# Homes of the large tiles: the same remainder modulo 128 in every pool

## The chip, the core and the metric

The kernel runs on one core of a Trainium2 chip. The metric is the device time of one execution in microseconds (us); lower is better. The core has TensorE (PE, matrix products; its weight loads are listed as PEld), VectorE (DVE), ScalarE (ACT), GpSimd (POOL) and the queues that issue DMA transfers (SP's above all). Operands lie in the on-chip memory SBUF, 128 partitions wide; a tile's home is the byte address in a partition at which it starts. Products land in the eight banks of PSUM.

## What is computed

A decoder trunk of two layers on x of shape (1, 512, 1024), all float32. Cut to what matters:

```python
def even_mixer(h, ...):                      # layer 0
    proj = h @ w_in; q, k, v, glu = split(proj)
    a = band_attention(rotary(q), rotary(k), v, window=127, sinks)   # 8 heads, 2 kv heads
    c = silu(layer_norm(causal_depthwise_conv(g_a * sigmoid(g_b)))) # 31 taps
    return concat([a, c]) @ w_out
def odd_mixer(h, ...):                       # layer 1
    proj = h @ w_in; q, k, v, z = split(proj)
    c_out = dilated attention, (window, dilation) (128,1), (512,4), (2048,16), mixed by denominators
    d_out = u * (spatial_w @ layer_norm(g) + spatial_b)             # u, g = split(gelu(z))
    return concat([c_out, d_out]) @ w_out
for layer in range(2):
    h = h + mixer[layer](rms_norm(h))
    h = h + (silu(n @ w_gate) * (n @ w_up)) @ w_down, n = rms_norm(h)   # 1024 -> 2816 -> 1024
return rms_norm(h)
```

## The kernel before

The residual h is kept as 8 tiles of 128 features x 512 tokens. Weights stream from memory in blocks of 128 x 1024 (raw). Each number is split in two parts of type float32r, a high and a low one: ACT writes the high part (w_hi, L174), DVE or POOL the difference (w_lo, L151). A product is three matmuls: high x high, low x high, high x low, with 512 columns moving and 128 x 128 stationary. `acc3` (L201 to L203) has the weights stationary (w_hi, w_lo) and the activations moving (xh, xl after a norm; oh, ol the mixer's output; hh, hl the FFN's hidden tiles; st and yc are homes that later oh and ol tiles reuse). `tok_gemm` (L262 to L264) has it the other way round. A weight load of the next matmul runs while the present one streams its columns.

The program's stages are: the first mixer (to about 196 us), the FFN of layer 0 (to about 560), the second mixer (to about 750), the FFN of layer 1 with the last norm. An FFN works in groups of four hidden tiles; the first group of two goes through `acc3`. For each of the later ones `product` makes seven products (a Strassen-like scheme) in which the weights' combination moves (w2h, w2l, L909 to L912) and the activations, either xh and xl or the prepared sums S1 to S4 (tiles s1 to s4), stand. Between the products stand down projections of the group before (`add_down`, 12 matmuls for each of 8 output tiles, result added to h in L939) and transposes (`turn`, L924) that need a PSUM bank which an add to h has to free. At the group's end ACT works a Silu (L997), then splits the next weights (L885), and DVE follows (L998, L151).

PE's order is written by hand: generators for attention and the conv's norm are stepped between matmuls by a clock of estimated costs (`C0`). The other engines' order is made by a scheduler from the order in which the code stands and from waits; equal code gives equal order.

Homes come from pools that are laid one behind the other in a partition: `const`, `keep` (h, xh, xl), `wpool` (raw, w_hi, w_lo), `scr` (scratch: ga, gb, small columns such as rl), and above them, one at a time, the pool of the stage: mix0, ffn, mix1. Each tile takes the next free place, rounded up to 32 bytes. The first large tiles lie at 96 above a multiple of 256. The stage pools begin at byte 111,392, which is 32 above a multiple of 256; in mix0 the score tiles Pm (two, of 8 rows of 257 columns) bring the tiles behind them to 160 above one.

Of the kernel before, what the change touches and what calls it, by code (L numbers as in the profile page):

```python
# [18 lines left out]
F32 = mybir.dt.float32  # L19
F32R = mybir.dt.float32r  # L20
AF = mybir.ActivationFunctionType
ALU = mybir.AluOpType

P = 128
# [110 lines left out]
def trunk_kernel(ctx: ExitStack, tc: tile.TileContext, xT, ws, cols, sinks, sgu_g, sgu_b,  # L135
                 spat_wT, spat_b, rope_c, rope_s, ident_d, mask0_d, mask1_d, fin_g, y):
    nc = tc.nc
    V, A, G, T = nc.vector, nc.scalar, nc.gpsimd, nc.tensor
# [5 lines left out]
    scr = ctx.enter_context(tc.tile_pool(name="scr", bufs=2))  # L144
    psum = ctx.enter_context(tc.tile_pool(name="psum", bufs=1, space=bass.MemoryType.PSUM))

    def bank(i, shape=None):
        return psum.tile(shape or [P, S], F32, name=f"bank{i}")
# [295 lines left out]
    with ExitStack() as mx:  # L444
        mp = mx.enter_context(tc.tile_pool(name="mix0", bufs=1))
# [5 lines left out]
        nc.sync.dma_start(sinkb, bass.AP(tensor=sinks.tensor, offset=sinks.offset, ap=[[0, P], [1, 8]]))  # L451
        nsink = mp.tile([P, 8], F32, name="nsink")
        V.tensor_scalar(out=nsink, in0=sinkb, scalar1=-1.0, scalar2=None, op0=ALU.mult)
        cp = [mp.tile([P, TAPS - 1 + S], F32, name=f"cp{j}") for j in range(4)]
        for j in range(4):
            G.memset(cp[j][:, 0:TAPS - 1], 0.0)
# [2 lines left out]
        V.tensor_scalar(out=taps, in0=taps, scalar1=0.5, scalar2=None, op0=ALU.mult)  # L459


        mp.tile([P, 8, 2 * P + 1], F32, name="Pm", bufs=2)
        for b in range(2):
            mp.tile([P, S], F32R, name=f"qs{b}", bufs=2)
        yc = [mp.tile([P, S], F32, name=f"yc{j}") for j in range(4)]
# [107 lines left out]
        def scores0(i):  # L573
            yield 0.0, C0["q"][i]
            while i >= 2 and ("V", i - 2) not in done:
                yield 0.0, 0.3
            qss = qTs[i]

            Pm = mp.tile([P, 8, 2 * P + 1], F32, name="Pm", bufs=2)
            A.activation(Pm[:, :, 2 * P:].rearrange("p (n b) o -> p n (b o)", b=2),  # L580
                         nsink[:, i:i + 5:4][:, None, :].to_broadcast([P, NQ, 2]), AF.Copy)
            nm = scr.tile([P, 8], F32, name="nm")
            l = scr.tile([P, 8], F32, name="l")
            for n2 in range(2):
                sb = [bank(2), bank(3)]
                for n1 in range(2):
                    n = 2 * n2 + n1
                    for b in range(2):
                        lo = max(n - 1, 0) * P
                        w = (n + 1) * P - lo  # L590
                        out = sb[b][:, n1 * 256 + 256 - w:n1 * 256 + 256]
                        q = slice(n * P, (n + 1) * P)
                        T.matmul(out, qss[b][:, q], khh[b][:, lo:lo + w], start=True, stop=False)
                        T.matmul(out, qss[b][:, q], kl[b][:, lo:lo + w], start=False, stop=True)
                for n1 in range(2):
                    n = 2 * n2 + n1
                    for b in range(2):
                        u = 2 * n + b
                        c0 = P if n == 0 else 0
                        hd = i + 4 * b  # L600
                        V.tensor_tensor_reduce(
                            out=Pm[:, u, c0:2 * P], in0=sb[b][:, n1 * 256 + c0:n1 * 256 + 256],
                            in1=mask0[:, c0:], scale=-0.125, scalar=nsink[:, hd:hd + 1],
                            op0=ALU.add, op1=ALU.min, accum_out=nm[:, u:u + 1])
                if n2 == 0:
                    yield 0.9, C0["S"]
            for u in range(8):
                c0 = P if u < 2 else 0
                A.activation(Pm[:, u, c0:], Pm[:, u, c0:], AF.Exp, bias=nm[:, u:u + 1], scale=-1.0,
                             accum_out=l[:, u:u + 1])  # L610
            rl = scr.tile([P, 8], F32, name="rl")
            V.reciprocal(rl, l)
            del qTs[i]
            pend[i] = Pm, rl, seq.t + 0.9 + C0["ST"]
            yield 0.9, 0.0
# [70 lines left out]
        for step in C0["steps"].split():  # L686
# [38 lines left out]
            if after:  # L725
                waiting.append(after)
                if len(waiting) > 1:
                    seq.until(lambda: "norm" in done)
                flush()
            elif kind == "L":  # L730
                seq.add("L", conv_norm())
            elif kind == "S":
                seq.add("S", scores0(i))
            elif kind == "V":
                seq.add("V", values0(i))
            elif kind == "Y":
                seq.until(lambda: all(("V", j) in done for j in range(4)))
                ps = bank(5)
                for k in range(4):
                    acc3(ps, (oh[k], ol[k]), k == 0, k == 3)  # L740
                early[i] = mp.tile([P, S], F32, name="prod", bufs=3)
                A.activation(early[i], ps, AF.Copy)
            else:
                if kind == "C":
                    break
                ns = {"A": C0["na"], "X": C0["nx"], "B": C0["na"] + C0["nx"]}[kind]
                k = i + 4 if kind == "B" else i
                seq.until(lambda: (("L" if kind == "B" else "V"), i) in done)
                for n in ns:
                    if n not in po:  # L750
                        po[n], ks[n] = bank(n), 0
                    ks[n] += 1
                    acc3(po[n], (oh[k], ol[k]), ks[n] == 1, ks[n] == 8)
# [313 lines left out]
    with ExitStack() as mx:  # L1067
        mp = mx.enter_context(tc.tile_pool(name="mix1", bufs=1))
# [67 lines left out]
        def scores1(i, qk, ql):  # L1136
            yield 0.0, C0["q1"]
            while i >= 2 and ("V1", i - 2) not in done:
                yield 0.0, 0.3
            Pm = [mp.tile([P, 10 * P], F32, name="Pm", bufs=3) for _ in range(2)]  # L1140
            nm = scr.tile([P, 8], F32, name="nm")
            rl = scr.tile([P, 8], F32, name="rl")
            for n in range(NQ):
                w = (n + 1) * P
                q = slice(n * P, w)
                sb = [bank(2), bank(3)]
                for b in range(2):
                    qs, ks = qk[b]
                    T.matmul(sb[b][:, :w], qs[:, q], ks[:, :w], start=True, stop=False)
                    T.matmul(sb[b][:, :w], ql[b][:, q], ks[:, :w], start=False, stop=True)  # L1150
                for b in range(2):
                    u = 2 * n + b
                    V.tensor_tensor_reduce(
                        out=Pm[b][:, offs[n]:offs[n] + w], in0=sb[b][:, :w],
                        in1=mask1[:, S - w:], scale=-0.125, scalar=3.0e38,
                        op0=ALU.add, op1=ALU.min, accum_out=nm[:, u:u + 1])
                    A.activation(Pm[b][:, offs[n]:offs[n] + w], Pm[b][:, offs[n]:offs[n] + w], AF.Exp,
                                 bias=nm[:, u:u + 1], scale=-1.0, accum_out=rl[:, u:u + 1])
                if n < NQ - 1:
                    yield 0.22 * (n + 1), C0["S1"]  # L1160
            V.reciprocal(rl, rl)
            pend[i] = Pm, rl, seq.t + 0.9 + C0["ST1"]
            yield 0.9, 0.0
# [22 lines left out]
        for i in range(4):  # L1186
            ps = gemm1(0)
            qT = mp.tile([P, S], F32, name="qT")
            rope(ps, qT, tabs)
            ps = gemm1(1)  # L1190
            kT = mp.tile([P, S], F32, name="kT")
            rope(ps, kT, tabs)
            seq.add("S1", scores1(i, *stack(i, qT, kT)))
            seq.add("V1", values1(i))
# [151 lines left out]
```

## Time and profile before

| | |
|---|---|
| runs | 1118.15, 1120.03, 1122.57 us; median 1120.03 |
| profiled execution | 1121.99 us, span 1120.3 us |
| mean granted clock of TensorE | 0.990 of full speed |
| busy: PE, DVE, ACT, POOL | 97%, 62%, 51%, 21% of the span |
| chain that ended last | PE 75%, DVE 11%, DMA 5%, ACT 4% |

Busy time is the time in which an engine works on at least one instruction. Matmuls are pipelined: each is shown for longer than it holds the array, so the distance between two starts is their pace, and the mean ns of a group goes up and down with it. In the table by stage each engine's busy time is followed by its count of instructions; behind the engines come the granted clock, the share of the 16 DMA engines and GB/s.

### The profile page before, as it was taken

What the parts mean: (1) busy time and instruction counts of PE and PEld (TensorE: products, weight loads), DVE (VectorE), ACT (ScalarE), POOL (GpSimd) and SP (SyncE); (2) the same over time, 40 slices, a digit from 0 to 9 for tenths busy, and PEclk for the clock granted to TensorE, in tenths of its full rate; (3) what the DMA queues carried; (4) which work ended last, traced back from release to release, by engine and by line L of the source; (5) the groups of instructions that cost most, each with busy time, mean ns of one, the idle gap of its engine ahead of it and who ended that gap; (6) DMA issues with size and microseconds to landing.
All of it is one profiled execution on the core that took longest, in us unless ns stands there. A gap on an engine that the chain in (4) does not pass through costs nothing.

```text
span 1120.3 us, 13714 instructions
## 1 busy us (share of the span) xinstructions
PE 1082.4 (97%) x5118; PEld 888.2 (79%) x5118; DVE 692.2 (62%) x1051; ACT 570.3 (51%) x930; POOL 233.3 (21%) x210
## 2 busy tenths in 40 slices
PE   9989889999999999999999999999999999999997
PEld 7877767878878888888887888787778788888785
DVE  3889966866565556564647647556665645555543
ACT  6577745754444353533546654446544443535433
POOL 0889944211101010100023300002111010101002
PEclk9989999999999999999998999999999999999999
DMA  6211113977767676611521111239877676666122
GB/s 230 69 57 62 46 57 112 273 204 179 187 151 167 175 150 188 135 35 63 168 90 57 57 57 58 82 111 263 213 179 185 151 169 186 139 192 141 27 68 76
DMA packets 42803, 145.89 MB, mean 130 GB/s; under 512 B 4848, under 2 KB 5744, under 8 KB 42736
## 3 DMA queue, kind: packets, MB, share of 16 engines
q1 hardware_dynamic: 30496, 100.88, 26.2%
q0 software_dynamic: 11520, 41.95, 21.9%
q10 hardware_dynamic: 720, 2.18, 0.6%
q8 instruction: 40, 0.66, 0.2%
q14 instruction: 27, 0.22, 0.1%
HBM read 142.89 MB, written 2.10 MB: 129 GB/s over the span
## 4 chain that ended last, share of the span: by engine, by line
PE 75%; DVE 11%; DMA 5%; ACT 4%; issue 3%; POOL 1%; POOLq 0%; ACTq 0%; SPq 0%
PE bank L911 10%; PE bank L912 10%; PE bank L909 10%; PE bank L201 10%; PE bank L202 10%; PE bank L203 10%; DMA raw<-in_ws 5%; DVE bank L483 3%; PE bank L262 2%; PE bank L264 2%; PE bank L263 2%; PE bank L421 2%; PE bank L924 1%; DVE w2l L151 1%; ACT w2h L885 1%
## 5 line engine op out<-in xcount | busy, mean ns | idle before, releaser
L151 DVE TENSOR_TENSOR w2l<-raw,w2h 128x1024 fp32r<-128x1024 f32 x140 | 171.2, 1225 | 209.0 <-ACT w2h L885 208.8
L885 ACT ACTIVATE w2h<-raw 128x1024 fp32r<-128x1024 f32 x140 | 147.7, 1058 | 213.6 <-PE bank L912 161.2
L174 ACT ACTIVATE w_hi<-raw 128x512 fp32r<-128x512 f32 x204 | 127.7, 628 | 193.0 <-PE bank L202 153.4
L875 POOL DMA_DIRECT2D raw<-in_ws x80 | 69.5, 877 | 560.2 <-DVE w2l L151 235.3
L151 DVE TENSOR_TENSOR w_lo<-raw,w_hi 128x512 fp32r<-128x512 f32 x164 | 117.1, 717 | 58.6 <-ACT w_hi L174 56.5
L911 PE MATMUL bank<-w2l,s 128*128 128x512 f32 x320 | 125.3, 391 | 2.6 <-DVE w2l L151 2.5
L909 PE MATMUL bank<-w2h,s 128*128 128x512 f32 x320 | 125.6, 393 | 1.4 <-DVE gb L845 1.3
L912 PE MATMUL bank<-w2h,s 128*128 128x512 f32 x320 | 124.9, 390 | 0.0
L201 PE MATMUL bank<-xh,w_hi 128*128 128x512 f32 x272 | 110.8, 407 | 1.1 <-ACT w_hi L174 1.1
L203 PE MATMUL bank<-xh,w_lo 128*128 128x512 f32 x272 | 107.6, 396 | 0.0
L202 PE MATMUL bank<-xl,w_hi 128*128 128x512 f32 x272 | 107.2, 394 | 0.0
L201 PE MATMUL bank<-hh,w_hi 128*128 128x512 f32 x256 | 101.4, 396 | 0.0
L203 PE MATMUL bank<-hh,w_lo 128*128 128x512 f32 x256 | 101.2, 395 | 0.0
L202 PE MATMUL bank<-hl,w_hi 128*128 128x512 f32 x256 | 101.2, 395 | 0.0
L909 PE MATMUL bank<-w2h,xh 128*128 128x512 f32 x240 | 95.7, 399 | 0.0
L911 PE MATMUL bank<-w2l,xh 128*128 128x512 f32 x240 | 94.8, 395 | 0.0
L912 PE MATMUL bank<-w2h,xl 128*128 128x512 f32 x240 | 94.8, 395 | 0.0
L911 PEld LDWEIGHTS bank<-w2l,s 128*128 128x128 f32 x320 | 60.1, 188 | 16.7 <-DVE w2l L151 4.1
L909 PEld LDWEIGHTS bank<-w2h,s 128*128 128x128 f32 x320 | 60.1, 188 | 15.1 <-DVE gb L845 1.7
L912 PEld LDWEIGHTS bank<-w2h,s 128*128 128x128 f32 x320 | 60.1, 188 | 12.6
L151 POOL TENSOR_TENSOR w_lo<-raw,w_hi 128x512 fp32r<-128x512 f32 x40 | 54.5, 1364 | 64.7 <-ACT w_hi L174 61.9
L939 DVE TENSOR_TENSOR h<-h,bank 128x512 f32<-128x512 f32 x69 | 47.1, 685 | 26.1 <-PE bank L203 26.1
(235 smaller groups left out, 2067.8 us busy)
## 6 DMA issues: line engine op xcount, KB each, us to landing
raw<-in_ws SPq DMA_DIRECT2D x177, 512.0 KB, 4.3
raw<-in_ws POOLq DMA_DIRECT2D x80, 512.0 KB, 5.7
h<-in_xT SPq DMA_DIRECT2D x8, 256.0 KB, 5.0
raw<-in_ws ACTq DMA_DIRECT2D x4, 512.0 KB, 4.6
out_y<-xh SPq DMA_DIRECT2D x4, 256.0 KB, 2.0
out_y<-xl SPq DMA_DIRECT2D x4, 256.0 KB, 2.3
raw<-in_ws SPq DMA_DIRECT2D x2, 256.0 KB, 4.0
ropeC<-in_rope_c SPq DMA_DIRECT2D x2, 256.0 KB, 4.1
```

Of the source, the lines that this page charges most:

```text
L151: eng.tensor_tensor(out=out, in0=a, in1=b, op=ALU.subtract)
L174: A.activation(hi, src, AF.Copy)
L201: T.matmul(ps, hi, xh, start=start, stop=False)
L202: T.matmul(ps, hi, xl, start=False, stop=False)
L203: T.matmul(ps, lo, xh, start=False, stop=stop)
L483: V.scalar_tensor_tensor(acc, src, w, acc, op0=ALU.mult, op1=ALU.add)
L875: nc.gpsimd.dma_start(t, ws[base + 8 * (g - 1) + 2 * BLOCK_OF[more] + q], accum_op=ALU.add)
L885: A.activation(hi, src, AF.Copy)
L909: T.matmul(ps[t], xh[:, c], wh[:, w], start=(start and j == 0), stop=False, skip_group_check=True)
L911: T.matmul(ps[t], xh[:, c], wl[:, w], start=False, stop=False, skip_group_check=True)
L912: T.matmul(ps[t], xl[:, c], wh[:, w], start=False, stop=(j == 3), skip_group_check=True)
L939: V.tensor_add(h[n], h[n], ps)
```

## The change

Four edits, all of them sizes. The two `rl` tiles of the scratch pool take 16 columns instead of 8 (64 bytes more in the pool, which moves every stage pool up by 64). In mix0 an unused tile of 16 columns is laid ahead of the conv's inputs cp. The rows of the scores Pm are 264 columns apart instead of 257 (224 bytes more in each of its two tiles); what is computed still uses columns 0 to 256, so the slices that ran to the row's end now name it.

No engine's instructions change in kind, number or order; one wait of SP's queue (a weight load L860 at the start of the first FFN) names instructions of DVE and PE that stand one and two places earlier. The homes become:

| tiles | remainder modulo 256 before | after |
|---|---|---|
| h, xh, xl, raw, w_hi, w_lo | 96 | 96 |
| scratch: ga, gb, R | 224 | 224 |
| ident, ones (small) | 32 | 32 |
| mix0: masks and rope tables | 32 | 96 |
| mix0: cp; qs, yc, prod, khh, kl, Vt, oh, ol, pts, on | 96 or 224; 160 | 224 or 96; 224 |
| mix0: rows of Pm | 1028 bytes apart | 1056 bytes apart |
| ffn: w2h, w2l, raw2, hh, hl, s1 to s4, ta, tb | 32 | 96 |
| mix1: all large tiles | 32 | 96 |
| nacc (end of the scratch pool) | 224 | 32 |

```diff
--- before.py
+++ after.py
@@ -451,6 +451,7 @@
         V.tensor_scalar(out=nsink, in0=sinkb, scalar1=-1.0, scalar2=None, op0=ALU.mult)
+        mp.tile([P, 16], F32, name="gap")
         cp = [mp.tile([P, TAPS - 1 + S], F32, name=f"cp{j}") for j in range(4)]
@@ -459,7 +460,7 @@
-        mp.tile([P, 8, 2 * P + 1], F32, name="Pm", bufs=2)
+        mp.tile([P, 8, 2 * P + 8], F32, name="Pm", bufs=2)
@@ -576,8 +577,8 @@
-            Pm = mp.tile([P, 8, 2 * P + 1], F32, name="Pm", bufs=2)
-            A.activation(Pm[:, :, 2 * P:].rearrange("p (n b) o -> p n (b o)", b=2),
+            Pm = mp.tile([P, 8, 2 * P + 8], F32, name="Pm", bufs=2)
+            A.activation(Pm[:, :, 2 * P:2 * P + 1].rearrange("p (n b) o -> p n (b o)", b=2),
@@ -606,9 +607,9 @@
-                A.activation(Pm[:, u, c0:], Pm[:, u, c0:], AF.Exp, bias=nm[:, u:u + 1], scale=-1.0,
+                A.activation(Pm[:, u, c0:2 * P + 1], Pm[:, u, c0:2 * P + 1], AF.Exp, bias=nm[:, u:u + 1], scale=-1.0,
                              accum_out=l[:, u:u + 1])
-            rl = scr.tile([P, 8], F32, name="rl")
+            rl = scr.tile([P, 16], F32, name="rl")[:, :8]
@@ -1139,7 +1140,7 @@
-            rl = scr.tile([P, 8], F32, name="rl")
+            rl = scr.tile([P, 16], F32, name="rl")[:, :8]
```

## Rows read from the trace of the kernel before

**Rows 1.** The profile's page, parts 1 and 4: busy us (share) xinstructions; the chain's shares.

```profile
PE 1082.4 (97%) x5118; PEld 888.2 (79%) x5118; DVE 692.2 (62%) x1051; ACT 570.3 (51%) x930; POOL 233.3 (21%) x210
...
PE 75%; DVE 11%; DMA 5%; ACT 4%; issue 3%; POOL 1%; POOLq 0%; ACTq 0%; SPq 0%
```

**Rows 2.** Table by stage: us, then busy us of PE, PEld, DVE, ACT, POOL, PEclk, DMA.

```profile
0.00:196.00 196.00, 177.97 (x909) 148.09 (x910) 148.44 (x274) 129.55 (x255) 125.32 (x102) 0.97 0.26 90
196.00:240.00 44.00, 42.97 (x194) 34.63 (x193) 33.99 (x49) 29.44 (x47) 8.31 (x9) 1.00 0.92 242
240.00:560.00 320.00, 318.61 (x1418) 259.07 (x1417) 187.06 (x237) 142.38 (x193) 28.70 (x33) 1.00 0.60 148
```

**Rows 3.** Single PE starts (start us, us), 914.8 to 922 us, second FFN.

```profile
915.47 0.40 PE L201 MATMUL bank<-hh,w_hi 128*128 128x512 f32 x1
...
918.27 0.39 PE L909 MATMUL bank<-w2h,s 128*128 128x512 f32 x1
...
919.65 0.39 PE L909 MATMUL bank<-w2h,s 128*128 128x512 f32 x1
...
921.92 0.39 PE L911 MATMUL bank<-w2l,s 128*128 128x512 f32 x1
```

**Rows 4.** Groups of PE's matmuls, 240 to 560 us: xcount | busy us, mean ns.

```profile
L201 PE MATMUL bank<-hh,w_hi 128*128 128x512 f32 x140 | 55.5, 397 | 0.0
L203 PE MATMUL bank<-hh,w_lo 128*128 128x512 f32 x140 | 55.4, 395 | 0.0
...
L909 PE MATMUL bank<-w2h,s 128*128 128x512 f32 x141 | 55.3, 392 | 0.0
...
L911 PE MATMUL bank<-w2l,s 128*128 128x512 f32 x141 | 55.0, 390 | 0.0
L909 PE MATMUL bank<-w2h,xh 128*128 128x512 f32 x112 | 44.6, 398 | 0.0
L911 PE MATMUL bank<-w2l,xh 128*128 128x512 f32 x112 | 44.2, 395 | 0.0
...
L201 PE MATMUL bank<-s,w_hi 128*128 128x512 f32 x32 | 12.6, 394 | 0.0
...
L264 PE MATMUL bank<-w_hi,xl 128*128 128x512 f32 x21 | 8.2, 389 | 0.0
```

**Rows 5.** Groups of PE's matmuls, 660 to 748 us, second mixer.

```profile
L203 PE MATMUL bank<-oh,w_lo 128*128 128x512 f32 x29 | 11.5, 396 | 0.0
L202 PE MATMUL bank<-ol,w_hi 128*128 128x512 f32 x29 | 11.5, 395 | 0.0
L201 PE MATMUL bank<-st,w_hi 128*128 128x512 f32 x28 | 11.1, 396 | 0.0
```

**Rows 6.** Groups of PE's matmuls, 1075 us to the end.

```profile
L262 PE MATMUL bank<-w_hi,s 128*128 128x512 f32 x32 | 12.6, 394 | 0.0
L264 PE MATMUL bank<-w_hi,s 128*128 128x512 f32 x32 | 12.5, 392 | 0.0
L263 PE MATMUL bank<-w_lo,s 128*128 128x512 f32 x32 | 12.4, 388 | 0.0
```

**Rows 7.** Waits of PE: who waited for whom: us in all, times, longest us.

```profile
PE bank L924 <- DVE h L939: 2.8, 8, 0.3
```

**Rows 8.** Groups of PE's matmuls, 140 to 196 us, first mixer.

```profile
L203 PE MATMUL bank<-oh,w_lo 128*128 128x512 f32 x58 | 22.8, 393 | 0.0
...
L202 PE MATMUL bank<-ol,w_hi 128*128 128x512 f32 x26 | 10.1, 389 | 0.0
```

**Rows 9.** Groups of ACT's copies, whole run.

```profile
L174 ACT ACTIVATE w_hi<-raw 128x512 fp32r<-128x512 f32 x204 | 127.7, 628 | 193.0 <-PE bank L202 153.4 <-PE bank L264 37.1 <-ACT sq L333 1.3
...
L827 ACT ACTIVATE s<-ga 128x512 fp32r<-128x512 f32 x8 | 4.9, 618 | 1.0 <-DVE ga L151 1.0
```

**Rows 10.** PE starts, with the idle time before them in brackets, near 68 us.

```profile
67.83 1.55 PE L421 MATMUL bank<-Vt,pts 128*128 128x64 f32 x7 [2.03 <-ACT pts L410]
```

**Rows 11.** Table by stage, columns as in Rows 2: the stretch behind that wait.

```profile
68.10:74.90 6.80, 6.80 (x32) 6.51 (x32) 3.94 (x6) 4.78 (x10) 6.72 (x6) 0.50 0.15 58
```

## Prediction

> **What bounds the kernel now.** I read the page's busy table and chain first, then the table by stage, then the matmuls grouped by operands in one stage, then single starts. TensorE is busy for 97% of the span and holds 75% of the chain that ended last [rows 1]. By stage the picture splits: in the long stretch of the first FFN, 240 to 560 us, PE is busy for 318.61 of 320 us, while in the first mixer, 0 to 196 us, it stands for 18 us, and at the first FFN's start the DMA engines are 92% busy [rows 2]. So a nanosecond per matmul is worth its full price in the FFNs and in the second mixer's end, little in the first mixer, and is doubtful in the first 40 us of an FFN.
>
> Matmuls overlap in the trace (each is shown at about 390 ns), so their pace is the distance between starts. In [rows 3] twelve matmuls of a down projection start between 915.47 and 918.27 us: 2.80 us, 233 ns each. Ten later ones, of a product, take from 919.65 to 921.92: 2.27 us, 227 ns each. Shape, types and the overlapped weight load are the same; the rows' duration follows the pace (395 or more against 389 to 390).
>
> What tells slow from fast is the pair of homes that TensorE reads. The three lines L909, L911, L912 run with the same moving tiles (w2h, w2l: 32 above a multiple of 256 before); with stationary s (also 32) they take 392, 390 and 390 ns, with stationary xh or xl (96) 398, 395 and 395 (L912, whose row isn't shown, reads as L911 in both) [rows 4]. Lines L201 to L203 with moving hh or hl (32) and stationary w_hi or w_lo (96) take 397, 395 and 395 (L202 reads as L203) [rows 4]. Both operands at 96 (w_hi moving, xl stationary) is 389 [rows 4]. So: equal remainders 389 to 392, remainders 64 bytes apart up to 398.
>
> **The change part by part.** It moves no instruction: every engine's list reads the same, tile by tile. What moves is addresses. The FFN and second mixer pools go from remainder 32 to 96, which is where xh, xl, w_hi and w_lo already are, so all pairs there become equal. In the first mixer the remainder modulo 128 becomes 96 too, but modulo 256 its tiles end at 224, 128 away from w_hi, a pair that no row of before has.
>
> Price of the unequal pairs, against the triple 392 + 390 + 390 = 1172 ns of L909, L911 and L912 with s:
> - FFN products with xh: three of seven products, 2 x 2 x 2 triples each, 10 groups: 240 triples. 398 + 395 + 395 = 1188, so 16 ns each: 3.84 us.
> - Down projections from hh: 8 x 18 in the first layer and 8 x 14 in the second: 256 triples. 397 + 395 + 395 = 1187, 15 ns each: 3.84 us. The first layer's last group (moving s) has 32 triples at 394 x 3 = 1182 [rows 4], 10 ns each: 0.32 us.
> - Second mixer's output projection: 32 triples with oh, ol at 396 and 395 for two of the three [rows 5]; L201 starts after a break in places, so I give it 6 ns, 17 ns in all: 0.54 us. 32 triples with st at 396 x 3 = 1188, 16 ns: 0.51 us.
> - Last down projection, w_hi and w_lo moving, hh and s stationary: 394 + 392 + 388 = 1174 [rows 6] against 3 x 389 = 1167 for the same form with xh or xl [rows 4], 7 ns, 64 triples: 0.45 us.
>
> Together 9.50 us. A second gain: after a slow run the pace takes six matmuls to settle, 918.27 to 919.65 us, 1.38 us against 6 x 227 = 1.36 [rows 3]. Four such switches in each of 10 groups: 0.8 us. Sum of gains: 10.3 us.
>
> What is given back. At a group's end TensorE runs a down projection of 12 matmuls while ACT and DVE work off a chain that does not get shorter (two Silu's, a w2h and its w2l, an add to h), then waits for that add: 8 times, 2.8 us in all [rows 7]. The 12 get 5 ns shorter each, so each wait grows by 0.06 us: 0.5 us. In the first 40 us of each FFN the DMA engines are at 92% [rows 2]; there some 36 unequal matmuls an FFN gain nothing if the loads set the pace: 72 x 5 ns = 0.36 us. Net 10.3 - 0.9 = 9.4, taken as 9.5 us.
>
> First mixer: 64 triples of oh with ol or yc are unequal now and stay so. They read 393 and 389 for two of the three [rows 8], so equal pairs would gain at most some 4 ns a matmul, and a pair as bad as the second mixer's (396, 395) would cost 3 to 6 ns: 192 x 4 = 0.8 us of gain to 192 x 6 = 1.2 us of loss. I take nothing, since the nearest row is its own, and since DVE and ACT set the pace there (TensorE stands for 18 us).
>
> Edits costed at nothing: ACT copies 512 columns in 628 ns from 96 to 96 and in 618 from 96 to 32 [rows 9], so ACT does not care which home it writes, and 10 ns on an engine that waits for TensorE would be hidden. The score rows, 264 instead of 257 columns apart, keep their element counts; the sink column is copied with a step of 1056 bytes instead of 1028. Both lie in the first mixer; the nearest bound is again those 10 ns, either way, on 32 scores and 32 exponentials: 0.6 us. nacc alone leaves 96 modulo 128 (for 32): 24 one-column matmuls. One weight load of the first FFN waits for slightly earlier instructions than before: it can only start earlier, into queues already full.
>
> The profiled execution took 1121.99 us (span 1120.3), 2 us above the median 1120.03. So the profiled time would become 1112.5 and the median **1110.5 us**.
>
> A rule that speaks against this. The Trainium skill, page "SBUF — State Buffer", section "Who interferes with whom", gives TensorE two independent read ports, one for the moving operand and one for weight loads, and says "PE and ACT never wait on anyone". By it the home of either operand is no matter, the change does nothing, and the time stays 1120.0. This case's trace disagrees as to the pace: L909 at 392 with s and 398 with xh [rows 4]. It ends where the first rival ends and has no chance beyond that one's.
>
> **The rivals.**
> *The remainder doesn't matter, the place does.* In this kernel everything at 96 lies in the first 110 KB of a partition and everything at 32 or 160 above it, so every unequal pair is also a pair from two regions. If it were the region that costs, the padding would do nothing: 1120.0 us. Against it: in both mixers oh (high) is multiplied with w_hi and w_lo (low) on the same lines, yet the first mixer's pairs, 64 apart the other way (160 and 96 modulo 256), read 393 and 389 [rows 8] and the second's (32 and 96) 396 and 395 [rows 5]. A cost that follows the remainder at one and the same distance of regions speaks for the remainder. For it: the stages differ in what else runs, so the contrast isn't pure.
>
> *The feeders take half of it.* If ACT, DVE and the loads were nearer to their limit than the table shows, the waits at group ends and at FFN starts would grow by more than the 0.9 us above. For 5 us of loss each of the 10 groups would have to wait 0.5 us more than now, where 0.3 is the longest now [rows 7]. DMA at 60% in the long stretch [rows 2] speaks against it. It gives 1115.5 us.
>
> *Slower, by the clock.* A wait of 2.03 us ends at 67.83 us [rows 10], and right behind it come 6.8 us at the lower clock level, 1.2 GHz (granted 0.50) [rows 11]. A TensorE that outruns its feeders waits more, and a fall at each of the 8 group ends would cost 8 x 3.4 = 27 us: 1120.0 - 9.5 + 27 = 1138 us. It decides once such a wait reaches the length of that one; now it is 0.3 us [rows 7], and 0.06 more is far from 2. Unlikely, but it is the one way to a loss that I can see.
>
> That the change doesn't do what it says: the homes of the built program are as said, save nacc and the 128 bytes in the first mixer.
>
> **How the numbers follow.** Forecast 0.74: equal pairs run at the pace of today's equal pairs, 1110.5 us. Its own range: down by 0.8 (first mixer), 3.4 (one fall of the clock less) and 0.8 (all equal pairs settled at 227) to 1105.5; up by 1.2 and 0.6 (first mixer) and 3.4 to 1115.5. The place 0.15 at 1120.0; the feeders 0.07 at 1115.5; the clock 0.04 at 1138. Range 1105.5 to 1119.5: it takes in nearly all of the forecast, the feeders and a part of the place. A measurement of this kernel tells 0.5%, 5.6 us, from no change: faster than 1114.4 is the forecast, 0.74; within 0.5% are the place and the feeders, 0.22; slower is the clock, 0.04.
>
> **What would show it.** Right: in the changed profile L909, L911 and L912 read the same, 389 to 392, with xh as with s; L201 to L203 with hh fall from 395 and more to about 390; twelve matmuls of a down projection take 2.72 us; the FFN's groups come 1 us closer, and the waits of L924 for h grow by less than 0.1 us each. Wrong: those rows still read 395 to 398 (the place), or they fall and the time doesn't, with longer waits at L909, L911 or L924 (the feeders) or granted clock under 1.00 in the FFNs (the clock). The first mixer's oh rows show what a distance of 128 does.

## The result, and the profile after

The change makes the kernel faster, by 11.6 us between the medians, where 9.5 were forecast.

| | before | after |
|---|---|---|
| runs, us | 1118.15 to 1123.71, median 1121.30 (4) | 1108.69 to 1110.73, median 1109.72 (4) |
| ratio after / before | | 0.990, 95% interval 0.987 to 0.993 |
| profiled execution, us | 1121.99 (span 1120.3) | 1110.54 (span 1108.8) |
| mean granted clock of TensorE | 0.990 | 0.994 |

The forecast was 1110.5 us, with a range from 1105.5 to 1119.5. The median of before is 1.3 us higher here than in the three runs that the forecast started from, because a fourth run was added. That the time came out within 0.8 us of the forecast is in part this: the gain was 2.1 us larger than forecast, and it was counted from a start that turned out 1.3 us higher.

The page, parts 1 and 4 as in [rows 1]: PE's busy time falls by 12.9 us, that of the weight loads by 2.1, and DVE's, ACT's and POOL's move by 1.1 at most. The chain leans more on PE, since DMA's share of it has gone from 5% to 3%.

```profile
PE 1069.5 (96%) x5118; PEld 886.1 (80%) x5118; DVE 691.1 (62%) x1051; ACT 570.8 (51%) x930; POOL 233.4 (21%) x210
...
PE 77%; DVE 11%; ACT 4%; DMA 3%; issue 2%; POOL 2%; POOLq 0%; ACTq 0%; DVEq 0%
```

In the table by stage (columns as in [rows 2]; the third stretch is taken to 550 us here, since the FFN ends 4 us earlier) the first mixer reads as before. The long stretch of the first FFN is as full of PE work as it was.

```profile
0.00:196.00 196.00, 177.45 (x905) 146.76 (x906) 148.21 (x273) 129.11 (x254) 125.39 (x101) 0.98 0.26 89
196.00:240.00 44.00, 43.14 (x196) 35.16 (x195) 34.44 (x50) 30.29 (x48) 8.58 (x9) 1.00 0.93 244
240.00:550.00 310.00, 307.74 (x1393) 254.22 (x1392) 184.61 (x235) 140.79 (x190) 28.18 (x33) 1.00 0.60 149
```

The single starts that answer to [rows 3] (start us, us; in the second FFN): twelve matmuls of a down projection take 909.25 - 906.53 = 2.72 us, where they took 2.80; the next ten, of a product, take 2.26, 226 ns each, from the first on. Nothing is left to settle. (In the kernel after, the lines of `product` and what follows are numbered one higher: L909, L911 and L912 of before are L910, L912 and L913, and L924 and L939 are L925 and L940.)

```profile
906.53 0.39 PE L201 MATMUL bank<-hh,w_hi 128*128 128x512 f32 x1
...
909.25 0.39 PE L910 MATMUL bank<-w2h,s 128*128 128x512 f32 x1
...
911.51 0.39 PE L912 MATMUL bank<-w2l,s 128*128 128x512 f32 x1
```

Groups of PE's matmuls in the first FFN, 230 to 550 us (xcount | busy us, mean ns of one), against [rows 4]: the products with xh read as those with s, and the down projections from hh have fallen from 397 and 395 to 391 and 389.

```profile
L910 PE MATMUL bank<-w2h,s 128*128 128x512 f32 x152 | 59.6, 392 | 0.0
L912 PE MATMUL bank<-w2l,s 128*128 128x512 f32 x152 | 59.3, 390 | 0.8 <-DVE w2l L151 0.8
...
L203 PE MATMUL bank<-hh,w_lo 128*128 128x512 f32 x143 | 55.7, 389 | 0.0
L201 PE MATMUL bank<-hh,w_hi 128*128 128x512 f32 x142 | 55.5, 391 | 0.6 <-DVE hl L151 0.6
L202 PE MATMUL bank<-hl,w_hi 128*128 128x512 f32 x142 | 55.4, 390 | 0.0
L910 PE MATMUL bank<-w2h,xh 128*128 128x512 f32 x112 | 44.0, 393 | 0.0
...
L912 PE MATMUL bank<-w2l,xh 128*128 128x512 f32 x112 | 43.6, 389 | 0.0
L201 PE MATMUL bank<-s,w_hi 128*128 128x512 f32 x32 | 12.4, 389 | 0.0
```

The same view of the second mixer, 650 to 735 us, against [rows 5]: 395 and 396 have become 389 and 390.

```profile
L202 PE MATMUL bank<-ol,w_hi 128*128 128x512 f32 x24 | 9.3, 390 | 0.0
L201 PE MATMUL bank<-st,w_hi 128*128 128x512 f32 x24 | 9.3, 389 | 0.0
...
L203 PE MATMUL bank<-oh,w_lo 128*128 128x512 f32 x24 | 9.3, 389 | 0.0
```

The last down projection, 1060 us to the end, against [rows 6]: 394 and 392 have become 389.

```profile
L262 PE MATMUL bank<-w_hi,s 128*128 128x512 f32 x32 | 12.4, 389 | 0.0
L263 PE MATMUL bank<-w_lo,s 128*128 128x512 f32 x32 | 12.4, 389 | 0.0
L264 PE MATMUL bank<-w_hi,s 128*128 128x512 f32 x32 | 12.4, 389 | 0.0
```

PE's waits for the add to h (us in all, times, longest) have grown from the 2.8 us of [rows 7] to 3.3, the longest from 0.3 to 0.4.

```profile
PE bank L925 <- DVE h L940: 3.3, 8, 0.4
```

And the first mixer, 140 to 196 us, where the pairs are now 128 bytes apart modulo 256 instead of 64: the 389 of [rows 8] reads 394.

```profile
L203 PE MATMUL bank<-oh,w_lo 128*128 128x512 f32 x58 | 22.9, 394 | 0.0
...
L202 PE MATMUL bank<-ol,w_hi 128*128 128x512 f32 x26 | 10.2, 394 | 0.0
```

### The profile page after: what moved, and what is told of

It reads as the page before. It is cut to its first block, busy times and chain, and to the rows that moved or that the text cites. A ratio compares the mean times of both kernels' runs of the same rounds, so it can differ in the third digit from the quotient of the medians.

```text
span 1108.8 us, 13714 instructions
## 1 busy us (share of the span) xinstructions
PE 1069.5 (96%) x5118; PEld 886.1 (80%) x5118; DVE 691.1 (62%) x1051; ACT 570.8 (51%) x930; POOL 233.4 (21%) x210
## 4 chain that ended last, share of the span: by engine, by line
PE 77%; DVE 11%; ACT 4%; DMA 3%; issue 2%; POOL 2%; POOLq 0%; ACTq 0%; DVEq 0%
PE bank L201 11%; PE bank L202 11%; PE bank L203 11%; PE bank L912 10%; PE bank L913 10%; PE bank L910 10%; DMA raw<-in_ws 3%; DVE bank L484 3%; PE bank L262 2%; PE bank L264 2%; PE bank L263 2%; PE bank L421 2%; DVE w2l L151 1%; PE bank L925 1%; ACT w2h L886 1%
## 5 line engine op out<-in xcount | busy, mean ns | idle before, releaser
L912 PE MATMUL bank<-w2l,s 128*128 128x512 f32 x320 | 125.0, 391 | 2.6 <-DVE w2l L151 2.5
L910 PE MATMUL bank<-w2h,s 128*128 128x512 f32 x320 | 125.6, 392 | 1.0 <-DVE gb L846 1.0
L913 PE MATMUL bank<-w2h,s 128*128 128x512 f32 x320 | 124.7, 390 | 0.0
L201 PE MATMUL bank<-xh,w_hi 128*128 128x512 f32 x272 | 111.3, 409 | 1.1 <-ACT w_hi L174 1.1
L203 PE MATMUL bank<-xh,w_lo 128*128 128x512 f32 x272 | 108.0, 397 | 0.0
L202 PE MATMUL bank<-xl,w_hi 128*128 128x512 f32 x272 | 107.8, 396 | 0.0
L201 PE MATMUL bank<-hh,w_hi 128*128 128x512 f32 x256 | 99.9, 390 | 0.6 <-DVE hl L151 0.6
L202 PE MATMUL bank<-hl,w_hi 128*128 128x512 f32 x256 | 99.8, 390 | 0.0
L203 PE MATMUL bank<-hh,w_lo 128*128 128x512 f32 x256 | 99.7, 389 | 0.0
L910 PE MATMUL bank<-w2h,xh 128*128 128x512 f32 x240 | 94.4, 393 | 0.0
L913 PE MATMUL bank<-w2h,xl 128*128 128x512 f32 x240 | 93.5, 390 | 0.0
L912 PE MATMUL bank<-w2l,xh 128*128 128x512 f32 x240 | 93.4, 389 | 0.0
L912 PEld LDWEIGHTS bank<-w2l,s 128*128 128x128 f32 x320 | 60.1, 188 | 16.2 <-DVE w2l L151 4.1
L910 PEld LDWEIGHTS bank<-w2h,s 128*128 128x128 f32 x320 | 60.1, 188 | 14.4 <-DVE gb L846 1.4
L913 PEld LDWEIGHTS bank<-w2h,s 128*128 128x128 f32 x320 | 60.1, 188 | 12.4
L201 PEld LDWEIGHTS bank<-xh,w_hi 128*128 128x128 f32 x272 | 52.3, 192 | 11.7 <-ACT w_hi L174 1.8
```

The costliest lines, as they stand in the source:

```text
L201: T.matmul(ps, hi, xh, start=start, stop=False)
L202: T.matmul(ps, hi, xl, start=False, stop=False)
L203: T.matmul(ps, lo, xh, start=False, stop=stop)
L910: T.matmul(ps[t], xh[:, c], wh[:, w], start=(start and j == 0), stop=False, skip_group_check=True)
L912: T.matmul(ps[t], xh[:, c], wl[:, w], start=False, stop=False, skip_group_check=True)
L913: T.matmul(ps[t], xl[:, c], wh[:, w], start=False, stop=(j == 3), skip_group_check=True)
```

## What the experiments had to settle

The theory is that of the prediction: what TensorE pays for is the difference, modulo 256, between the home of the tile that streams and the home of the tile from which weights are loaded; at difference 0 it pays nothing. The rivals: the place in memory and not the remainder; the value 96 itself; another of the four edits (score rows, padding in the mixer). Four questions were asked, and in all of these kernels every engine's instructions stand in the same order; only homes differ.

The edits that follow are against the kernel after, but for the second, which is against the kernel before. For the pace I took, from the trace, the distance between the starts of neighbouring 512-column matmuls and its mean over all pairs of one difference (moving home minus home of the weights loaded beside it, which are those of the next matmul, modulo 256), leaving out distances of 245 ns and more.

### Which part of the change does it: the value, the padding, the mixer

**All homes rigidly elsewhere.** 48 more columns in the lowest pool bring every large tile that lay at 96 to 32, and the first mixer's from 224 to 160: all differences stay.

```diff
     V.memset(mhalf, -0.5)
+    const.tile([P, 48], F32, name="shift")
```

> The changed kernel with 192 bytes more at the end of the const pool: every tile behind it moves rigidly, so the large tiles of all pools stand 32 above a multiple of 256, equal to each other as in the changed kernel but at the remainder that the FFN tiles had before. Equal remainders are what counts: the same as the changed kernel, 1110 us (1107 to 1113), L910 with xh at 392 to 393 ns, L201 with hh at 389 to 390. The remainder 96 itself is what counts (32 is a slow home): all pairs at 395 or more, about 3700 matmuls x 6 ns over the changed kernel's pace, 1130 us. The place in the partition is what counts: not excluded by this run alone, since distances stay; it too gives 1110.

Measured: 1110.04 us (1109.06 to 1112.91), ratio to before 0.991 (0.988 to 0.994). The pace of equal pairs is 227.19 ns over 3765 matmuls; in the kernel after it is 227.18 over 3757. So 96 is no special home. Equality is what counts. The line of `product` with xh (L911 here is L910 after, which read 393; 230 to 550 us):

```profile
L911 PE MATMUL bank<-w2h,xh 128*128 128x512 f32 x112 | 44.0, 393 | 0.0
```

**The padding of rl alone**, on the kernel before: 64 bytes more in the scratch pool, no padding in the mixer, score rows as they were.

```diff
-            rl = scr.tile([P, 8], F32, name="rl")
+            rl = scr.tile([P, 16], F32, name="rl")[:, :8]
...
-            rl = scr.tile([P, 8], F32, name="rl")
+            rl = scr.tile([P, 16], F32, name="rl")[:, :8]
```

> Only the rl edit on the kernel before: 64 bytes more in the scratch pool, so FFN and second mixer go from 32 to 96 while the score rows stay 257 columns apart. If the pairs of the FFN and the second mixer are all of the gain: 1110 us as the changed kernel (1107 to 1113). If the score rows' 264 columns or the first mixer's other paddings bring part of it: later than the changed kernel by that part, up to 1115. The place rival expects no change, 1121 us.

Measured: 1109.87 us (1108.58 to 1115.58), ratio 0.990 (0.987 to 0.993), equal pairs at 227.24 ns. Two sizes in the scratch pool are the whole gain. The score rows and the mixer's padding bring nothing that can be told from it.

**The first mixer made equal too.** 128 bytes ahead of its masks lift its large tiles from 224 to 96 modulo 256.

```diff
+        mp.tile([P, 32], F32, name="gap0")
```

> The changed kernel with 128 bytes ahead of the first mixer's tiles, so that they too stand 96 above a multiple of 256 and no longer 128 bytes away from w_hi and w_lo. Remainder modulo 256: the pairs of oh, ol and yc with w_hi and w_lo in the first mixer fall from a pace of 232 to 227 ns, L202 with ol from about 395 to 389 ns; 192 matmuls x 5 ns = 1 us if TensorE sets the pace there, nearer 0.3 us with DVE and ACT setting it: 1109.4 (1106 to 1112). Remainder modulo 128 is all that counts: those rows do not move.

Measured: 1109.43 us (1106.14 to 1114.10), ratio 0.990 (0.987 to 0.994): the same time. The row moved as the theory says. Here are two groups of PE's matmuls, 140 to 196 us; the second line is the one that read 394:

```profile
L203 PE MATMUL bank<-oh,w_lo 128*128 128x512 f32 x58 | 23.1, 399 | 0.0
...
L202 PE MATMUL bank<-ol,w_hi 128*128 128x512 f32 x26 | 10.1, 390 | 0.0
```

The first line doesn't show it, because this execution had 3.4 us at the lower clock level in that stretch (the granted clock, the last column but two in the table by stage):

```profile
166.80:170.20 3.40, 3.40 (x10) 2.66 (x9) 0.69 (x1) 1.41 (x2) 1.31 (x2) 0.50 0.44 154
```

Leaving such stretches out, the pace there falls from 232.24 ns (165 matmuls 128 apart, in the kernel after) to 227.63 (158 matmuls), some 0.7 us in all. In these homes the first mixer's tiles and the weights still differ by 256 bytes modulo 512, and the pairs pay next to nothing; so do w2h, w2l and xh, xl in the run that follows (227.0 to 227.6 ns). So the period is 256 at most. That the time doesn't follow is no surprise for 0.7 us among runs that scatter by 8.

### One operand out of line

**w_lo alone at 160** (96 everywhere else), so that in `acc3` one weight load in three is 64 off.

```diff
+        if u == 0:
+            wpool.tile([P, 16], F32, name="gap2", bufs=1)
...
+        if u == 0:
+            wpool.tile([P, 48], F32, name="gap3", bufs=1)
```

> The changed kernel with the four homes of w_lo alone moved 64 bytes up (160 above a multiple of 256), all else in place. In acc3 a matmul of L202 streams xl (96) while w_lo (160) is loaded for the next one, and a matmul of L203 streams xh (96) with w_lo standing while w_hi (96) is loaded. If what collides is the stream with the NEXT matmul's weight load: L202 becomes longer (389 to about 395 ns) and L203 stays at 389 or 390. If it is the stream with its own weights' home: L203 becomes longer and L202 stays. Time: 688 triples x about 6 ns = 4 us over the changed kernel, about 1114 us (1111 to 1117), in both cases; the place rival expects 1110 (no change).

Measured: 1116.52 us (1114.68 to 1123.64), ratio 0.9969 (0.9945 to 0.9993): of some 12 us gained, 5 remain. In the first FFN, 230 to 550 us, the lines that read w_lo are slow again and the products, which don't read it, are not (L205 to L207 here are L201 to L203, L916 is L912):

```profile
L916 PE MATMUL bank<-w2l,s 128*128 128x512 f32 x152 | 59.3, 390 | 0.1
...
L207 PE MATMUL bank<-hh,w_lo 128*128 128x512 f32 x144 | 57.1, 397 | 0.0
L206 PE MATMUL bank<-hl,w_hi 128*128 128x512 f32 x143 | 56.2, 393 | 0.7 <-DVE hl L368 0.7
L205 PE MATMUL bank<-hh,w_hi 128*128 128x512 f32 x143 | 55.8, 391 | 0.0
```

The triple is 391 + 393 + 397 = 1181 against 391 + 390 + 389 = 1170 after and 1187 before [rows 4]: one pair out of line in three costs 11 of the 17 ns that three cost, not a third. Neither answer of the expectation is the whole of it: L203's row grew by 8 ns and L202's by 3. By the starts the odd matmul itself is 7.8 ns longer, the one ahead of it 1.9 and the one behind it 1.5, over some 563 triples with a clean stretch around them: 563 x 11.2 = 6.3 us, of the 6.8 by which this kernel is above the one after.

**xl alone at 160**, which is a moving tile in `acc3` and a stationary one in `product`.

```diff
+        if xs[k] is None:
+            keep.tile([P, 16], F32, name=f"gapa{k}")
...
+        if xs[k] is None:
+            keep.tile([P, 48], F32, name=f"gapb{k}")
```

> The changed kernel with the eight homes of xl alone moved 64 bytes up (160 above a multiple of 256). Two places tell in which row a collision is shown. In acc3 with xh and xl all loads (w_hi, w_hi, w_lo) stand at 96 and only L202's stream is odd: whatever it collides with, it does so in L202. If the cost of a collision is shown in the row of the stream that collides, L202 with xl gets longer (389 to 393 or more) and L203 stays; if it is shown one matmul later, L203 gets longer. In the products with xh the load of xl for L913 is odd, as w_lo's was in the run before: if the pattern there was general, L912 becomes some 4 ns and L913 some 8 ns longer. Time: 240 triples x 13 ns plus about 200 triples x 6 ns: about 4 us over the changed kernel, 1114 us (1111 to 1117).

Measured: 1116.47 us in one run (before beside it 1122.27). In the products with xh the pattern is that of the run before, as expected: 8 ns more for the matmul on xl and 3 for the one ahead of it (250 to 550 us; L917 and L916 are L913 and L912 of after, both 389 there).

```profile
L917 PE MATMUL bank<-w2h,xl 128*128 128x512 f32 x112 | 44.4, 397 | 0.0
L916 PE MATMUL bank<-w2l,xh 128*128 128x512 f32 x112 | 43.9, 392 | 0.0
```

In `acc3` these pairs were equal before the change and after it, in the same place, and they become slow when one tile moves by 64 bytes. In the second mixer's projection (655 to 741 us) these two lines read 390 after. Both rows grew by 4 ns, so they don't tell in which row a collision is shown:

```profile
L203 PE MATMUL bank<-xh,w_lo 128*128 128x512 f32 x32 | 12.6, 394 | 0.0
L202 PE MATMUL bank<-xl,w_hi 128*128 128x512 f32 x32 | 12.6, 394 | 0.0
```

**Both at 160**, to learn which load a streaming tile collides with: the one for the next matmul, which goes on beside it, or its own. The edit for w_lo is the one above; for xl, the tiles are claimed in another order so that the padding stands around all of xl:

```diff
+    for k in range(KT):
+        keep.tile([P, S], F32R, name=f"xh{k}")
+    keep.tile([P, 16], F32, name="gapa")
+    for k in range(KT):
+        keep.tile([P, S], F32R, name=f"xl{k}")
+    keep.tile([P, 48], F32, name="gapb")
```

> The changed kernel with w_lo and xl both moved 64 bytes up (160 above a multiple of 256), xh and w_hi left at 96. In acc3 with xh and xl every stream then has the remainder of the NEXT matmul's weights (xh before a load of w_hi, xl before a load of w_lo), while two streams of three differ from their OWN weights (xl on w_hi, xh on w_lo). If the stream collides with the load that runs beside it, L202 and L203 with xl and xh are back at 389 to 391 ns, less than with either of the two moves alone (394 and 394 with xl moved). If it is the own weights' home that counts, they are at 395 or more. Down projections (hh, hl, s at 96) see w_lo alone moved and read as with that move alone: 391, 393, 397. Time: down projections 288 triples x 13 ns and products with xl 240 x 13 ns over the changed kernel, 6 to 7 us: 1116 us (1113 to 1119) by the first theory, 2 us more by the second.

Measured: 1123.33 us in one run (before beside it 1121.78). The second mixer's projection, 655 to 741 us (L206 and L207 are L202 and L203 of after):

```profile
L206 PE MATMUL bank<-xl,w_hi 128*128 128x512 f32 x32 | 12.6, 393 | 0.0
L207 PE MATMUL bank<-xh,w_lo 128*128 128x512 f32 x32 | 12.5, 392 | 0.0
```

This is neither the 389 to 391 of the first answer nor the 395 and more of the second, and the time fits neither.

The starts say more. With w_lo alone moved, matmuls whose own weights stand 64 above the stream go at 235.1 ns (563) and those whose own weights are equal to it at 228.3 (3074); sorted by the next matmul's weights instead, the two groups are the same, 229.3 and 229.3 (616 and 3021). With xl alone it is 235.0 against 228.1 by the own weights and 229.5 against 228.6 by the next. So in these two runs the loss stands in the row of the matmul whose own weights are out of line. With both moved this fails as well: outside the first mixer xh on w_lo, 64 away, goes at 229.6 ns (127), and xh on w_hi, with both its own and the next weights at its own remainder, at 232.3 (129; after: 227.7). So no single pair decides, and a difference of 0 to the weights is not enough when other tiles nearby are out of line. What exactly collides stays open. The theory is only as sharp as this: where all the tiles have equal homes, matmuls run at 227 ns, and a tile out of line costs.

### How far out of line: the ladder

One unused tile at the head of the ffn pool and one in mix1 lift the tiles of the FFNs and of the second mixer by X bytes, with everything else as after. 16 columns are 64 bytes; 32, 8, 24 and 40 columns give 128, 32, 96 and 160.

```diff
+            fp.tile([P, 16], F32, name="gap1")
...
+        mp.tile([P, 16], F32, name="gap1")
```

64 bytes:

> The changed kernel with 64 bytes ahead of the tiles of both FFNs and the second mixer: they stand 160 above a multiple of 256, 64 above xh and w_hi, where before they stood 64 below. If the pace depends on the signed distance modulo 256, as the first mixer's rows of before suggest (64 above: 229 ns): L201 to L203 with hh at about 391 ns on average, and the time 1968 matmuls x 2 ns = 4 us over the changed kernel, 1114 us (1111 to 1117). If only the distance modulo 128 counts and the first mixer's rows were lower because other work runs there: rows at 395 to 398 as before, 1120 us. The last down projection, where the low tiles move, sees the distance from the other side: 233 ns by the first theory, 229 by the second.

128 bytes:

> The changed kernel with 128 bytes ahead of the tiles of both FFNs and the second mixer: they stand 224 above a multiple of 256, 128 away from xh and w_hi. If the pace depends on the distance modulo 256, as the first mixer's rows of the changed kernel say (128 away: 232 ns): L201 to L203 with hh at 394 or more, time 1968 x 5 ns = 10 us over the changed kernel, 1119 us (1116 to 1123). If the distance modulo 128 is what counts: 389 to 390, 1110 us.

32 bytes:

> The changed kernel with 32 bytes ahead of the tiles of both FFNs and the second mixer: they stand 128 above a multiple of 256, 32 above xh and w_hi. No row has this distance. If the pace changes in steps of 64 bytes, it is that of an equal pair or of 64 above: 227 to 229 ns, rows at 389 to 391, time 1110 to 1114 us. If it goes with the distance in smaller steps or each odd distance costs the full price: rows of 393 to 398, 1115 to 1121 us.

96 bytes:

> The changed kernel with 96 bytes ahead of the tiles of both FFNs and the second mixer: 96 above xh and w_hi. By the runs before (equal 227 ns, 64 above 229, 128 away 232.5, 64 below 233, 32 away 233) only equal and 64 above are cheap: full price, 233 ns, L202 and L203 with hh at 394 to 396, 1120 us (1117 to 1123). If the price falls off evenly between 64 above and 128: about 231 ns, 1117 us.

160 bytes:

> The changed kernel with 160 bytes ahead of the tiles of both FFNs and the second mixer: 160 above, or 96 below, xh and w_hi. By the same reading full price: 233 ns, L202 and L203 with hh at 394 to 396, 1120 us (1117 to 1123). The last down projection sees 96 above here.

Measured, with the kernels after and before as the rows 0 and 192. The second column is the down projection from hh in the first FFN (250 to 550 us, for 0 and 192 as quoted), the third the mean distance between starts over all pairs of that difference, outside the first mixer but for the row 0, which has its equal pairs too. In these kernels all weights of a triple have one home, so the own and the next matmul's weights can't be told apart here:

| moving home minus weights' home, modulo 256 | L201 + L202 + L203 with hh, ns | pace, ns (matmuls) | time, us |
|---|---|---|---|
| 0 (after) | 391 + 390 + 389 | 227.2 (3757) | 1109.72 |
| 32 | 397 + 396 + 394 | 233.3 (1748) | 1120.86, one run |
| 64 | 393 + 395 + 389 | 229.0 (1749) | 1114.88, one run |
| 96 | 395 + 400 + 392 | 233.5 (1750) | 1124.32, one run |
| 128 | 397 + 396 + 394 | 232.4 (190 of the last down projection), 232.5 (1914 with the first mixer's) | 1120.09, one run |
| 160 | 398 + 397 + 396 | 234.1 (1749) | 1124.49, one run |
| 192 (before) | 397 + 395 + 395 | 233.2 (1753) | 1121.30 |
| 224 | | 233.3 (190, last down projection of the kernel with 32) | |

The pace, not the time, is what orders these: a single run can be some us off (13 runs of before: 1118.80 to 1126.40). The kernels with 96 and 160 bytes came out 1.3 and 1.5 us above the ranges expected of them, and two of their rows with hh, 400 and 392 with 96 bytes, outside the expected 394 to 396; the full price was right. Two things stand out. All differences but 0 and 64 cost much the same, 5 to 7 ns. And the sign counts. The cheap 64 is a mean of unlike lines (250 to 550 us; by the starts 231.6, 229.1 and 226.2 ns):

```profile
L202 PE MATMUL bank<-hl,w_hi 128*128 128x512 f32 x136 | 53.7, 395 | 0.0
L201 PE MATMUL bank<-hh,w_hi 128*128 128x512 f32 x136 | 53.5, 393 | 0.0
L203 PE MATMUL bank<-hh,w_lo 128*128 128x512 f32 x136 | 52.9, 389 | 0.0
```

With X = 64 the down projections from hh stream from 64 above the weights, at 229.0; the last down projection, in the same kernel, streams w_hi from 64 below the stationary s, and reads 394 (1065 us to the end; 389 after):

```profile
L264 PE MATMUL bank<-w_hi,s 128*128 128x512 f32 x32 | 12.6, 394 | 0.0
...
L263 PE MATMUL bank<-w_lo,s 128*128 128x512 f32 x32 | 12.6, 394 | 0.0
```

By the starts that is 233.2 ns over 190 matmuls. Before the change it was the other way round, 233.2 for hh and 229.1 for the last down projection, with the same two pools: the difference of the homes goes with the pace, and the stage doesn't. The 128-byte kernel's rows for hh and xh (250 to 550 us) show that being equal modulo 128, as the change's title has it, isn't enough:

```profile
L201 PE MATMUL bank<-hh,w_hi 128*128 128x512 f32 x136 | 54.1, 397 | 1.2 <-DVE hl L151 1.2
L202 PE MATMUL bank<-hl,w_hi 128*128 128x512 f32 x136 | 53.8, 396 | 0.0
...
L913 PE MATMUL bank<-w2l,xh 128*128 128x512 f32 x112 | 44.2, 395 | 0.0
```

## Why the prediction was right, point by point

**What bounds the kernel.** TensorE, and there the distance between starts: confirmed. Only matmuls changed their pace, and the span went with PE's busy time (11.5 us of span, 12.9 of busy).

**The unequal pairs, 9.5 us.** Right, and low. The triples with xh and with hh have lost 17 ns each (1188 to 1171, 1187 to 1170) where 16 and 15 were taken; st has lost 21 (1188 to 1167) for 16, s in the first layer's last group 15 (1182 to 1167) for 10, the last down projection 7 as taken. The reference triple of 1172 ns was 1 to 5 ns too long: equal pairs now read 1171 in the products, 1170 from hh and 1167 from s. Counted from the starts, each matmul against itself: 1749 went from 233.2 to 226.9 ns and 190 from 229.1 to 227.2, 11.1 + 0.4 = 11.4 us.

**Settling, 0.8 us.** The right mechanism, and too small. Before, equal pairs had a mean pace of 228.1 ns, although most of them ran at 226 and 227; the same 1816 matmuls go at 227.4 after: 1.2 us. Nearly all of it, 1.1 us, is in the first eight equal pairs behind a switch: 282 matmuls at 230.7 ns before and 226.9 after. From the eleventh on they read 226.9 in both. The prediction looked at one switch, from a down projection into a product, and found 0.02 us in it, where the mean is 0.03; for forty switches it took 0.8.

**Given back at the group ends, 0.5 us.** As forecast: eight waits for h, 2.8 us before and 3.3 after. The group's beat (first transposes of one group to those of the next, by their starts) went from 63.3 to 62.3 us, the 1 us that the prediction gave as a sign, in all groups but the first FFN's first, which the next point is about.

**Given back at the FFN's start, 0.36 us.** The mechanism holds, but the place was another and the term too small. The stretch from 196 to 240 us is as full of DMA as before (0.93), and the kernel gained 1.0 us by 262 us all the same. Then 1.1 us was lost in one place, near 281 us. ACT waits there for a block of weights, 3.24 us where it waited 2.00 before; so hh and hl, which it and DVE write next, come later than TensorE wants them, and TensorE waits, which it didn't before. First the row of before, then two of after (start us, us, with the idle time in brackets):

```profile
277.96 1.06 ACT L885 ACTIVATE w2h<-raw 128x1024 fp32r<-128x1024 f32 x1 [2.00 <-DMA raw<-in_ws]
```

```profile
278.86 1.06 ACT L886 ACTIVATE w2h<-raw 128x1024 fp32r<-128x1024 f32 x1 [3.24 <-DMA raw<-in_ws]
...
281.93 0.47 PE L201 MATMUL bank<-hh,w_hi 128*128 128x512 f32 x1 [0.58 <-DVE hl L151]
```

The rigid shift, the rl padding alone and the kernel with an equal first mixer have the same differences of homes in that stage; at these matmuls they lose 0.3 to 0.6 us, with waits of ACT of 2.4 to 2.7 us. So a part goes with the change: a faster TensorE comes to a place where the loads set the pace. How much of the 1.1 us is scatter, one execution of each can't tell.

**Edits costed at nothing.** Right as far as the rows show: ACT's busy time in all grew by 0.5 us and DVE's fell by 1.1. The reading behind it was not: ga, from which the copies of 618 ns come, stands at 224 modulo 256 and not at 96. When the home of s went from 32 to 96, the copy (L828 after) went from 618 to 620, so the 10 ns of [rows 9] don't come from the home that is written.

```profile
L828 ACT ACTIVATE s<-ga 128x512 fp32r<-128x512 f32 x8 | 5.0, 620 | 1.0 <-DVE ga L151 1.0
```

**The first mixer, taken as 0, between 0.8 of gain and 1.2 of loss.** The unseen difference of 128 costs: 232.2 ns against the 229.0 of before, 165 x 3.2 = 0.5 us of loss in its matmuls. The stage ended 1.0 us later in the profiled execution, but 1.5 us had been lost in its first 30 us, where no pair of large tiles differs from before, and 1.0 returned by other stretches at the lower clock. With the rl padding alone, where the same pairs are 128 apart, it lost 0.2 us in its first 30 and 0.6 by its end. Repairing it gave no time that could be told. To call it nothing was right to within what can be measured.

**What came from elsewhere.** The profiled execution came out 2 us lower than the 1112.5 forecast for it. 11.4 + 1.2 - 0.5 (first mixer) - 0.5 (h) - 1.1 (near 281 us) = 10.5 us is what the terms of the prediction explain of the 11.5. The forecast's 9.4 took both its gains (10.3, measured 12.6) and its losses (0.9, measured 2.1) too small, errors that in part cancelled. Of the rest I can name pieces of both signs: 1.5 us lost at the start and 1.0 returned, as told above, and the clock. (The upper end of the forecast's own range adds up to 1115.7, not 1115.5.) After PE's wait for st in the second mixer (2.64 us before, 2.66 after) it went at 1.2 GHz for 6.8 us before and 3.4 after, by the granted clock in the table by stage; by the starts of the matmuls that is worth 1.35 us. First the row of before, then that of after:

```profile
590.30:597.10 6.80, 6.33 (x17) 5.17 (x18) 3.87 (x8) 2.55 (x7) 1.55 (x1) 0.50 0.22 77
```

```profile
587.50:590.90 3.40, 3.40 (x9) 2.63 (x8) 2.32 (x7) 2.26 (x7) 0.33 (x1) 0.50 0.43 140
```

The wait is as long in both. In the traces of the other kernels the stretch at that place is 0 us (128 bytes), 3.4 or 6.8 us long (xl alone) behind waits of 2.5 to 3.2 us, so this is scatter between executions and not the change. It is part of why runs of one kernel differ by several us.

**The rule against it.** The Trainium skill, page "SBUF — State Buffer", section "Who interferes with whom", has TensorE's two read ports as independent and says that PE and ACT never wait on anyone. This case's runs disagree as to PE. Had the homes been no matter, the time would have stayed at 1120.0; a matmul takes 227.2 ns at equal homes and 229.0 to 234.1 at others, and the kernel 1109.72 us for 1121.30. What the two reads share can't be seen in a trace.

**The rivals.** *The place, not the remainder* (0.15) is refuted: 64 bytes in the scratch pool, which leave every tile in its region, give the whole gain, and 32 or 128 bytes more in the stage's pool take nearly all of it away. The argument that the prediction had against it, that the first mixer's pairs at 64 the other way were cheap, was sound: the ladder shows 229.0 for 64 above and 233.2 for 64 below. *The feeders take half*: they took 0.5 us at the group ends, the longest wait 0.4, and up to 1.1 us near 281 us, far from 5. *The clock*: no wait for h is longer than 0.4 us, and the granted clock is 1.00 in the first FFN's stretches.

## What to carry to other kernels

Where TensorE streams matmuls of this form (512 columns, float32r, a 128 x 128 weight load for each) back to back, give all tiles that it reads the same home modulo 256: a few columns of padding in a lower pool can do it, and here they were worth 1% of the time. Other forms and types were not tried. The difference is what counts, so look at the groups of matmuls by operands: if lines that do the same work differ by 5 ns or more with the names of their operands, compare the homes. Check the difference modulo 256 and not 128, and in all pools, because one tile out of line cost 11 of the 17 ns that three cost.

## What the runs showed that was not expected

- The cost is signed and has one step that is cheap in the mean: 64 above costs 1.8 ns a matmul, 64 below 6.0, 32 and 96 above 6.1 and 6.3, 128 costs 5.3, 160 above 6.9.
- One weight load in three out of line costs 11 of the 17 ns of a whole triple, spread over its neighbours. Where w_lo moves instead of standing, it costs more alone than with its neighbours: in the last down projection 231.0, 232.1 and 232.6 ns on the three lines with w_lo alone 64 above, and 231.7, 226.0 and 229.0 before, where w_hi and w_lo both were. Two tiles moved together (w_lo and xl) give a value between (393 and 392) that neither simple picture of the collision explains. That stays open.
- Even at equal homes 512 columns take 227.2 ns in the mean, most of them 226 or 227. The Trainium skill, page "TensorE: Matmul & The Clock Gate", section "Back-to-back issue gap", gives about 216 ns for matmuls by themselves and about 131 for a stream with weight loads. This case's traces don't agree with the second figure: nothing here, in float32r and with a weight load each, comes near it.
- No cost of the homes of ACT's and DVE's operands shows in these traces: a copy of ACT that was moved from 32 to 96 changed by 2 ns.
